# Second feed-forward of an encoder block: four combined pairs of chunks, two block sums of each by accumulating transfers, and the second half of its input copied by ScalarE

## The chip, the cores and the metric

The kernel runs on one core of one Trainium2 chip. Five engines take part: TensorE (PE in the profile, its weight loads PEld), VectorE (DVE), ScalarE (ACT), GpSimd (POOL) and SyncE (SP). SP and POOL issue the DMA transfers used here. The metric is the device time of one execution in microseconds (us); lower is better.

## The reference

One layer of a streaming-encoder block, in single precision, on a sequence of 256 frames of width 1024: a feed-forward, a mixer of a gated recurrence and a forgetting attention, a cross-attention to a memory of 256 frames, and a second feed-forward, each with a norm before and behind it. The change touches only the last step:

```python
def swiglu(h, w_in, w_down):
    gate, up = jnp.split(h @ w_in, 2, axis=-1)
    return (jax.nn.silu(gate) * up) @ w_down
...
        h = rmsnorm(x, ffn2_pre_g[l])
        x = x + 0.5 * rmsnorm(swiglu(h, ffn2_w_in[l], ffn2_w_down[l]), ffn2_post_g[l])
```

Here w_in is 1024 x 5632 and w_down 2816 x 1024.

## The kernel before

**Numbers.** Every fp32 operand is split into a high part (rounded to the fp32r type that TensorE multiplies) and a low part (the rest). ScalarE makes the high part by a cast and VectorE the low part by a subtraction: lines 153 and 155 for a weight tile as it is loaded (`load_split`), 173 and 174 in `split` for all else. A product is three matmuls of 512 columns: high by high, high by low, low by high. A weight tile, a "unit", is 128 x 1024, that is two blocks of 128 rows by 512 columns.

**The feed-forward.** `ffn` is called for both feed-forwards, `f1_in` and `f2_in` in the tables. The hidden width 2816 is cut into 11 chunks of 256 (`NFF`). A chunk's input weights are four units; they give 512 columns, the gates and the ups of the chunk. The 256 frames are two halves (h) of 128. There are three ways to do a chunk. By tokens (`act_tok`, the table `TOKS`): for each half 8 blocks of the width times 3 matmuls, so 24 matmuls, 48 for the chunk. By columns (`act_col`), used for no chunk in question. As a pair with the next chunk (`act_pair`, the table `PAIRS`): the two token halves, the two halves of the width and the two chunks make a 2 x 2 by 2 x 2 block product, which is done in the way of Strassen and Winograd with seven products in place of eight. Each is 12 matmuls, so a pair has 84 where two chunks by tokens have 96. Its price is sums of weight blocks, which are split like weights.

**A pair in order.** `sums` holds block (0, 0) plus further blocks as the pair goes on, `both` a sum of blocks (0, 1) and (1, 1) (the first number is the half of the width, the second tells the chunk, 1 for the pair's first and 0 for its second). Each is two tiles of the "extra" buffers (4 in all); other blocks of a pair are loaded into "raw" buffers (4 in all). The seven products are, with their stationary input: p1 from the plain input, b4 from "de", then on top of p1's bank "aed", on b4's bank "baed", on p1's bank "ad", a new bank b0 from the second half of the width, and "e" on p1's bank. Each is preceded by the splits (`splits`) of two tiles, a cast and a subtraction of 128 x 1024 for either. `add` (line 596) does the block sums on VectorE. `more` (line 569) loads a block; with an operation it is an accumulating transfer issued by POOL, which adds the block to what the tile holds. With `FETCHED` the (1, 1) block comes into `both` that way.

**Outputs.** ScalarE takes copies of p1, v, w and p5, and VectorE combines them to the output quarters c01, c11, c00; the last one is the bank of "e" itself. `act_evac` applies the silu (`sg`, ScalarE, line 450) and multiplies by the up part (`at`, VectorE, lines 453 and 455). `flush` transposes the `at` tiles of a chunk (line 445) and splits them into `acts`, the input of the second product.

**The second product.** `down(c, h)` is 12 matmuls, two of them a chunk. They are put between the products of a pair (`step_between`); the last ones, of chunks 7 to 10, follow at the end. Before, the second feed-forward does chunks 0, 1, 2 by tokens, then pair 3 (chunks 3 and 4, with downs 0 to 2 in between), chunk 5 by tokens, pair 6 (downs 3 to 5), chunk 8 by tokens, and pair 9 (down 6).

**The input.** `X4` is the normed input of the second feed-forward, transposed. Before, it is a `Joined`, with high and low parts side by side, filled by `gain_split` (lines 372 and 373) one 128 x 128 block after another: TensorE transposes four blocks into a bank, ScalarE casts each with the gain of its rows, VectorE subtracts. The second half of the frames is done by `second`, whose transpositions are put in the order among the matmuls of the first half (`after(m + L_F2)`). `pair_joined` adds the parts back together for the pairs, 128 x 512 at a time, and `pair_inputs` forms "de", "aed", "ad", "baed" from that.

**Order.** Instructions of each engine run in a fixed order, made by a scheduler from the order of the code, with `after`, `issue_after` and `high_priority` as bounds. Loads are in SP's order, the accumulating transfers in POOL's.

Of the kernel before, what the change touches and what calls it, by code (L numbers as in the profile page):

```python
# [11 lines left out]
F32 = mybir.dt.float32  # L12
F32R = mybir.dt.float32r
I32 = mybir.dt.int32
AF = mybir.ActivationFunctionType
ALU = mybir.AluOpType
AX = mybir.AxisListType

P = 128
D = 1024  # L20
T = 256
# [11 lines left out]

STAG = 3

TOKS = {"f1_in": (3, 8), "f2_in": (2, 5, 8)}

PAIRS = {"f1_in": (4, 6, 9), "f2_in": (3, 6, 9)}

L_ACT = 21  # L40
L_F1 = 24
# [4 lines left out]
L_F2 = 36  # L46
# [6 lines left out]
M_T = (103, 115)  # L53
M_O = (126, 130)

FETCHED = {"f1_in": (4, 6, 9), "f2_in": (3, 6, 9)}
R_AT = (66, 130, 188, 252, 286, 332)

FG = 3
# [26 lines left out]
def block_kernel(ctx: ExitStack, tc: tile.TileContext, wts, head_in, gf_in, x_in, mem_in, memT_in, cols, rows, fbias, masks, out):  # L86
    nc = tc.nc
    V, S, G, PE = nc.vector, nc.scalar, nc.gpsimd, nc.tensor
# [13 lines left out]
    @contextmanager  # L102
    def after(i):

        with tc.high_priority(), tc.issue_after(log[min(i, len(log) - 1)]):
            yield
# [7 lines left out]
    def m4(shape, dt=F32, n="m"):  # L114
        return mp.tile(shape, dt, tag="m4", name=nm(n))
# [10 lines left out]
    def trp():  # L126
        return pp.tile([P, 512], F32, tag="tr", name=nm("tr"), bufs=2)
# [8 lines left out]
    evicted = []  # L136
# [35 lines left out]
    def split(hi, lo, src):  # L172
        a = S.copy(hi, src)  # L173
        b = V.tensor_tensor(out=lo, in0=src, in1=hi.bitcast(F32), op=ALU.subtract)  # L174
        return a.ins, b.ins

    class Pair:
# [7 lines left out]
        def more(self):  # L185
            self.h.append(m4([P, 4, T], F32R, "hT"))
            self.l.append(m4([P, 4, T], F32R, "lT"))
# [71 lines left out]
    ident = cp.tile([P, P], F32, name="ident")  # L259
# [4 lines left out]
    cols_s = cp.tile([P, 64], F32, name="cols_s")  # L264
# [4 lines left out]
    G_F1, G_MIX, G_MEM, G_KV, G_F2, G_HG, C_LB = 0, 8, 16, 24, 32, 40, 48  # L269
# [63 lines left out]
    def rstd_x(src, into=None, act=False):  # L333

        s = s1(2, name="ss2")
        for j in range(2):
            ssq(s[:, j : j + 1], src[j])
            if act and j == 0:
                b = sums_of(s)
        if not act:  # L340
            return rstd_of(s, into=into)
        r = s1(name="rstd") if into is None else into
        V.tensor_scalar(out=r, in0=step(*root(s, b)), scalar1=-16.0, scalar2=None, op0=ALU.mult)
        return r
# [6 lines left out]
    def fac_of(i, h):  # L351
        return fac[i][:, 32 * h : 32 * h + 1]

    def x_halves(h):
        return [xs[:, h, 0:512], xs[:, h, 512:]]
# [33 lines left out]
    def x_blocks(h):  # L389
        return lambda kb: xs[:, h, kb * P : (kb + 1) * P]  # L390
# [36 lines left out]
    def ffn(w_in, w_dn, X, r2, n_tok, i_row, first_half, second_half=None):  # L427
# [87 lines left out]

        def pair_joined(k):
            t = m4([P, 4, T], n="xf")
            for i in range(2):  # L520
                x = X.t[2 * k + i].bitcast(F32)
                V.tensor_tensor(out=t[:, 2 * i : 2 * i + 2], in0=x[:, :, 0], in1=x[:, :, 1], op=ALU.add)
            return t

        def ratio():

# [44 lines left out]
        def act_pair(c, between):  # L571
            sx, q, more_parts = pairs_in
# [7 lines left out]
            def splits(t):  # L580
                u = []
                for r in t:
                    p = parts_of()
                    split(p[0], p[1], r)
                    u.append(p)
                return u
# [7 lines left out]
            def add(t, o):  # L594
                for x, y in zip(t, o):
                    V.tensor_tensor(out=x, in0=x, in1=y, op=ALU.add)  # L596
# [15 lines left out]
            sums, both = sums_of_pair.pop(c)  # L612
# [19 lines left out]
            raw = raws(1, 1)  # L632
            add(sums, raw)
            u = splits(sums)
            if "e" not in sx:
                more_parts("ad", "e")
            product(b1, of("aed"), u, False)
# [5 lines left out]
            with tc.high_priority():  # L643
                t = half_tile("c01")
# [4 lines left out]
            with tc.high_priority():  # L649
                t = half_tile("c11")  # L650
# [4 lines left out]
            raw = raws(1, 0)  # L655
            m = len(log)
            product(b0, of_x(1), splits(raw), True)
            add(sums, raw)
            with tc.high_priority():
                t = half_tile("c00")  # L660
                V.tensor_tensor(out=t, in0=p1, in1=b0, op=ALU.add)
# [25 lines left out]
        pairs, pairs_in = PAIRS[w_in], None  # L687
        for c in range(n_tok):
            acts[c] = m4([P, 2, 2, T], F32R, "act")
        for h in range(2):  # L690
            m = len(log)
            for c in range(n_tok):
                act_tok(c, h)
            if h == 0 and n_tok:
                second_half(m)
                q, row = ratio()
                if pairs:
                    xf = [pair_joined(k) for k in range(2)]
        accs = None
        done = 0  # L700
        if callable(r2):
# [3 lines left out]
            q, row = ratio()  # L705
# [8 lines left out]
        for c in range(n_tok, NFF):  # L714
# [17 lines left out]
            elif c == 2 and first_half:  # L732
                n = len(log)
# [45 lines left out]
        m = len(log)  # L779
# [68 lines left out]
    def half(X, r, h, g, *ms, into=None, act=True):  # L848

        for i, m in enumerate(ms):  # L850
            with after(m):
                to_T(X, x_blocks(h), h, g, (i,) if len(ms) == 2 else (0, 1), mm if X is X3 and h else trp)
        r[h] = rstd_x(x_halves(h), into, act)
# [537 lines left out]
    def add(t, o):  # L1391
        for x, y in zip(t, o):
            V.tensor_tensor(out=x, in0=x, in1=y, op=ALU.add)  # L1393
# [303 lines left out]
        hold[_AT["mo"] + kb] = marks[(1, 1, 3, 3)[kb]]  # L1697
    for i in range(2):
        place[_AT["f2_in"] + i] = [wp.tile([P, D], F32R, tag="extra", name=nm("w"), bufs=4) for _ in range(2)]
    X4 = Joined()  # L1700
    r4 = [None, None]
    po = [[acc(), acc()], [acc(), acc()]]
    for kb in range(3):
# [12 lines left out]


    def second(m):
        half(X4, r4, 1, G_F2, m + L_F2, into=fac_of(3, 1), act=False)

    ffn("f2_in", "f2_dn", X4, r4, 2, 3, None, second)

# [90 lines left out]
```

## Time and profile before

| | us |
|---|---|
| median of 3 runs | 766.29 |
| the 3 runs | 765.70, 766.29, 767.17 |
| the profiled execution, its own time | 767.82 |
| its span in the profile | 765.6 |
| granted clock, mean | 0.998 |
| TensorE busy | 756.7 (99%) |
| VectorE busy | 664.4 (87%) |
| ScalarE busy | 521.2 (68%) |
| GpSimd busy | 33.0 (4%) |

The profiled execution is one run of its own, and its span leaves out 2.2 us of that time at the start and the end. Busy shares are means over the span; a stage can be bound by another engine than the whole. The chain of waits follows back from the last instruction to what released it. In a group's row stand line, engine and operation, output and inputs by the program's names, shapes, the count, busy us, and the mean ns of one instruction, then the idle time ahead of them and what ended it. In a row of the timeline stand the start in us, the duration, the engine, the line, the operation and, in brackets, the idle time ahead and its releaser.

### The profile page before, as it was taken

Reading aid. Unit: us, or ns where it says so; the run is one execution under the profiler, and the core shown is the slowest. Engines: PE = TensorE matmul, PEld = TensorE weight load, DVE = VectorE, ACT = ScalarE, POOL = GpSimd, SP = SyncE. Lnnn points to the kernel's source line nnn. Section 1 sums busy time; section 2 is a strip of 40 time slices with the busy share of each in tenths; the row PEclk is TensorE's granted clock in tenths of the full one; section 3 lists DMA queues with packets and bytes.
Section 4 is the critical chain, followed back from the end, with each engine's and each line's share of the span. In section 5 each row is a group of like instructions: output and inputs, shape, how many; then the busy total and the mean of one; then the engine's idle time right before and its main releaser. Section 6 shows DMA issues by size and latency. Waiting matters only on the chain.

```text
span 765.6 us, 11756 instructions
## 1 busy us (share of the span) xinstructions
PE 756.7 (99%) x4302; PEld 642.8 (84%) x4302; DVE 664.4 (87%) x982; ACT 521.2 (68%) x841; POOL 33.0 (4%) x56
## 2 busy tenths in 40 slices
PE   9999999999999999999999999999999999999996
PEld 8888888888888998898888888888887888888885
DVE  6799998988678898888689899999979899997973
ACT  8667576688774659667666755875968566675762
POOL 0000000000000100200001000001000100000000
PEclk9999999999999999999999999999999999999999
DMA  9778777674745545835668955586386837868641
GB/s 350 235 259 245 214 239 275 182 252 167 233 158 149 185 137 183 284 128 182 189 220 245 267 183 186 175 286 131 114 291 191 257 108 257 236 222 269 176 131 55
DMA packets 47146, 157.88 MB, mean 206 GB/s; under 512 B 5385, under 2 KB 9105, under 8 KB 47089
## 3 DMA queue, kind: packets, MB, share of 16 engines
q1 hardware_dynamic: 43168, 144.83, 55.5%
q0 software_dynamic: 3488, 11.94, 8.7%
q8 instruction: 33, 0.54, 0.3%
q10 hardware_dynamic: 432, 0.37, 0.2%
q14 instruction: 25, 0.20, 0.1%
HBM read 156.06 MB, written 1.06 MB: 205 GB/s over the span
## 4 chain that ended last, share of the span: by engine, by line
PE 85%; DVE 8%; ACT 2%; DMA 2%; issue 1%; DVEq 0%; ACTq 0%
PE mm L100 45%; PE acc L100 33%; PE tr L100 5%; DVE lo L155 2%; DMA raw<-in_wts_dram 2%; PE tr L445 1%; DVE lo L174 1%; ACT hi L153 1%; PE tr L385 1%; DVE xs L421 1%; DVE sraw L1393 1%; DMA head<-in_head_dram 0%; DVE post L416 0%; DVE sx L174 0%; DVE qm L1578 0%
## 5 line engine op out<-in xcount | busy, mean ns | idle before, releaser
L155 DVE TENSOR_TENSOR lo<-raw,hi 128x1024 fp32r<-128x1024 f32 (+1 forms) x188 | 222.3, 1199 | 29.5 <-ACT hi L153 26.2
L153 ACT CAST hi<-raw 128x1024 fp32r<-128x1024 f32 (+1 forms) x188 | 190.9, 1033 | 50.3 <-DMA raw<-in_wts_dram 29.7
L100 PE MATMUL mm<-hi,hlT 128*128 128x512 f32 (+1 forms) x632 | 191.6, 382 | 0.0
L100 PEld LDWEIGHTS mm<-hi,hlT 128*128 128x128 f32 x632 | 116.7, 188 | 20.2
L100 PE MATMUL mm<-lo,hlT 128*128 128x512 f32 (+1 forms) x316 | 119.1, 381 | 0.0
L100 PE MATMUL acc<-hi,act 128*128 128x512 f32 x352 | 113.6, 390 | 0.0
L173 ACT CAST hi<-sraw 128x1024 fp32r<-128x1024 f32 x80 | 83.3, 1052 | 33.9 <-DVE sraw L596 15.6
L174 DVE TENSOR_TENSOR lo<-sraw,hi 128x1024 fp32r<-128x1024 f32 x80 | 96.1, 1221 | 3.8 <-ACT hi L173 3.4
L100 PE MATMUL mm<-hi,sx 128*128 128x512 f32 x280 | 90.8, 391 | 0.0
L100 PEld LDWEIGHTS acc<-hi,act 128*128 128x128 f32 x352 | 66.2, 188 | 13.4
L100 PE MATMUL acc<-lo,act 128*128 128x512 f32 x176 | 69.5, 395 | 0.0
L100 PEld LDWEIGHTS mm<-lo,hlT 128*128 128x128 f32 x316 | 59.3, 188 | 10.0
L100 PEld LDWEIGHTS mm<-hi,sx 128*128 128x128 f32 x280 | 52.5, 188 | 10.9
L100 PE MATMUL acc<-hlT,hi 128*128 128x512 f32 x240 | 60.7, 394 | 0.0
L100 PE MATMUL mm<-lo,sx 128*128 128x512 f32 x140 | 54.9, 392 | 0.0
L100 PEld LDWEIGHTS acc<-hlT,hi 128*128 128x128 f32 x240 | 43.1, 189 | 7.7 <-DVE hlT L373 0.2
L174 DVE TENSOR_TENSOR lo<-raw,hi 128x1024 fp32r<-128x1024 f32 x32 | 38.6, 1221 | 2.1 <-ACT hi L173 2.0
L173 ACT CAST hi<-raw 128x1024 fp32r<-128x1024 f32 x32 | 33.1, 1053 | 8.5 <-issue 3.1
L100 PEld LDWEIGHTS acc<-lo,act 128*128 128x128 f32 x176 | 33.1, 188 | 6.4
L100 PE MATMUL acc<-lo,hT 128*128 128x512 f32 x96 | 37.8, 393 | 0.0
L100 PE MATMUL acc<-hi,hT 128*128 128x512 f32 x96 | 37.7, 392 | 0.1
L100 PE MATMUL acc<-hi,lT 128*128 128x512 f32 x96 | 37.3, 391 | 0.0
(329 smaller groups left out, 1232.4 us busy)
## 6 DMA issues: line engine op xcount, KB each, us to landing
raw<-in_wts_dram SPq DMA_DIRECT2D x215, 512.0 KB, 4.6
sraw<-in_wts_dram SPq DMA_DIRECT2D x32, 512.0 KB, 6.6
sraw<-in_wts_dram POOLq DMA_DIRECT2D x20, 512.0 KB, 5.9
raw<-in_gf_dram SPq DMA_DIRECT2D x12, 344.0 KB, 3.7
head<-in_head_dram SPq DMA_DIRECT2D x7, 392.0 KB, 6.4
grow<-in_rows_dram SPq DMA_DIRECT2D x4, 512.0 KB, 7.6
xs<-in_x_dram SPq DMA_DIRECT2D x2, 512.0 KB, 7.6
cb<-cd POOLq DMA_DIRECT2D x2, 512.0 KB, 4.9
```

Of the source, the lines that this page charges most:

```text
L100: log.append(PE.matmul(*args, **kw).ins)
L153: casts.append(S.copy(h, r).ins)
L155: los.append(V.tensor_tensor(out=l, in0=r, in1=h.bitcast(F32), op=ALU.subtract).ins)
L173: a = S.copy(hi, src)
L174: b = V.tensor_tensor(out=lo, in0=src, in1=hi.bitcast(F32), op=ALU.subtract)
L385: PE.transpose(blocks[-1][1], src(kb), ident)
L421: summed = V.scalar_tensor_tensor(out=xh, in0=ts[a // 512][:, a % 512 : (b - 1) % 512 + 1], scalar=r, in1=xh, op0=ALU.mult, op1=ALU.add)
L445: PE.transpose(trv[:, j, h * P : (h + 1) * P], ats[c, h][:, j * P : (j + 1) * P], ident)
L1393: V.tensor_tensor(out=x, in0=x, in1=y, op=ALU.add)
```

## The change

In the second feed-forward the chunks 5 and 8 are no longer done by tokens: chunks 3 to 10 are four pairs, 3, 5, 7 and 9. Pair 3 has the downs 0 to 2 in between, pair 5 the downs 3 and 4, pair 7 the downs 5 and 6, and pair 9 none. In each pair the block (1, 0) is added to `sums` by an accumulating transfer of POOL, issued behind the splits for "aed" (`FETCHED_LAST`), where VectorE added a loaded copy. `X4` is a `Pair`, with the high and the low parts in tiles of their own. `second` now transposes a block, lets ScalarE copy it with its gain to an fp32 tile `xf4`, and splits four blocks at once. `joined` writes the first half of `xf4` as the sum of high and low parts, one instruction for four blocks.

```diff
--- before.py
+++ after.py
@@ -33,9 +33,9 @@
 
 STAG = 3
 
-TOKS = {"f1_in": (3, 8), "f2_in": (2, 5, 8)}
-
-PAIRS = {"f1_in": (4, 6, 9), "f2_in": (3, 6, 9)}
+TOKS = {"f1_in": (3, 8), "f2_in": (2,)}
+
+PAIRS = {"f1_in": (4, 6, 9), "f2_in": (3, 5, 7, 9)}
 
 L_ACT = 21
 L_F1 = 24
@@ -53,7 +53,8 @@
 M_T = (103, 115)
 M_O = (126, 130)
 
-FETCHED = {"f1_in": (4, 6, 9), "f2_in": (3, 6, 9)}
+FETCHED = {"f1_in": (4, 6, 9), "f2_in": (3, 5, 7, 9)}
+FETCHED_LAST = {"f1_in": (), "f2_in": (3, 5, 7, 9)}
 R_AT = (66, 130, 188, 252, 286, 332)
 
 FG = 3
@@ -515,12 +516,9 @@
 
 
 
-        def pair_joined(k):
-            t = m4([P, 4, T], n="xf")
-            for i in range(2):
-                x = X.t[2 * k + i].bitcast(F32)
-                V.tensor_tensor(out=t[:, 2 * i : 2 * i + 2], in0=x[:, :, 0], in1=x[:, :, 1], op=ALU.add)
-            return t
+        def joined(k):
+            hi, lo = (t[k].bitcast(F32)[:, :, :P] for t in (X.h, X.l))
+            V.tensor_tensor(out=xf4[k][:, :, :P], in0=hi, in1=lo, op=ALU.add)
 
         def ratio():
 
@@ -632,6 +630,9 @@
             raw = raws(1, 1)
             add(sums, raw)
             u = splits(sums)
+            if c in FETCHED_LAST[w_in]:
+                for j in range(2):
+                    more(sums[j], c, 1, 0, j, ALU.add)
             if "e" not in sx:
                 more_parts("ad", "e")
             product(b1, of("aed"), u, False)
@@ -655,7 +656,8 @@
             raw = raws(1, 0)
             m = len(log)
             product(b0, of_x(1), splits(raw), True)
-            add(sums, raw)
+            if c not in FETCHED_LAST[w_in]:
+                add(sums, raw)
             with tc.high_priority():
                 t = half_tile("c00")
                 V.tensor_tensor(out=t, in0=p1, in1=b0, op=ALU.add)
@@ -694,8 +696,9 @@
             if h == 0 and n_tok:
                 second_half(m)
                 q, row = ratio()
-                if pairs:
-                    xf = [pair_joined(k) for k in range(2)]
+                xf = xf4
+                for k in range(2):
+                    joined(k)
         accs = None
         done = 0
         if callable(r2):
@@ -1697,7 +1700,8 @@
         hold[_AT["mo"] + kb] = marks[(1, 1, 3, 3)[kb]]
     for i in range(2):
         place[_AT["f2_in"] + i] = [wp.tile([P, D], F32R, tag="extra", name=nm("w"), bufs=4) for _ in range(2)]
-    X4 = Joined()
+    X4 = Pair()
+    xf4 = [m4([P, 4, T], n="xf") for _ in range(2)]
     r4 = [None, None]
     po = [[acc(), acc()], [acc(), acc()]]
     for kb in range(3):
@@ -1716,7 +1720,16 @@
 
 
     def second(m):
-        half(X4, r4, 1, G_F2, m + L_F2, into=fac_of(3, 1), act=False)
+        for q in range(2):
+            x = xf4[q][:, :, P:]
+            ps = trp()
+            with after(m + L_F2):
+                for j in range(4):
+                    kb = 4 * q + j
+                    PE.transpose(ps[:, j * P : (j + 1) * P], x_blocks(1)(kb), ident)
+                    S.activation(x[:, j], ps[:, j * P : (j + 1) * P], AF.Copy, scale=cols_s[:, G_F2 + kb : G_F2 + kb + 1])
+                evicted.append(split(X4.h[q][:, :, P:], X4.l[q][:, :, P:], x))
+        r4[1] = rstd_x(x_halves(1), fac_of(3, 1))
 
     ffn("f2_in", "f2_dn", X4, r4, 2, 3, None, second)
 
```

The order of instructions moves at three places. In the rows, numbers behind names tell tiles of one name apart.

TensorE where the second half of the input is made, `tr` being the banks of the transpositions, `mm` the bank of the first half's chunk 1. Before:

```order
L100 MATMUL mm_6239<-hi_6253,hlT_5960 128x512
L385 MATMUL tr_6292<-ident,xs 128x128 x4
L385 MATMUL tr_6297<-ident,xs 128x128 x4
L100 MATMUL mm_6239<-lo_6254,hlT_5960 128x512
L100 MATMUL mm_6239<-hi_6253,hlT_5960 128x512 x2
```

Now:

```order
L101 MATMUL mm_6241<-hi_6255,hT_5960 128x512
L1729 MATMUL tr_6294<-ident,xs 128x128
L1729 MATMUL tr_6305<-ident,xs 128x128
L101 MATMUL mm_6241<-lo_6256,hT_5960 128x512
L101 MATMUL mm_6241<-hi_6255,lT_5961 128x512
L1729 MATMUL tr_6294<-ident,xs 128x128
L101 MATMUL mm_6241<-hi_6255,hT_5960 128x512
L1729 MATMUL tr_6305<-ident,xs 128x128
```

Eight transpositions stood together; now the two banks take turns, with matmuls in between.

VectorE at the start of pair 9. Before, 7354 and 7356 are pair 9's `sums`, 7358 and 7360 its `both`:

```order
L174 TENSOR_TENSOR lo_7418<-sraw_7354,hi_7417 128x1024
L596 TENSOR_TENSOR sraw_7354<-sraw_7354,raw_7457 128x1024
L174 TENSOR_TENSOR lo_7422<-sraw_7356,hi_7421 128x1024
L174 TENSOR_TENSOR lo_7464<-sraw_7354,hi_7463 128x1024
L453 TENSOR_TENSOR at_7352<-mm_7325,sg_7350 128x256
L596 TENSOR_TENSOR sraw_7356<-sraw_7356,raw_7458 128x1024
L596 TENSOR_TENSOR sraw_7354<-sraw_7354,raw_7538 128x1024
L174 TENSOR_TENSOR lo_7468<-sraw_7356,hi_7467 128x1024
```

Now, 7415 and 7417 are its `sums`; the `at` tile 7413 is of pair 7's last product:

```order
L454 TENSOR_TENSOR at_7382<-c_1562_7378,sg_7380 128x256
L175 TENSOR_TENSOR act_7140<-tr_7404,act_7140 128x512
L456 SCALAR_TENSOR_TENSOR at_7413<-mm_7144,q_6334,sg_7411 128x256
L175 TENSOR_TENSOR lo_7462<-sraw_7415,hi_7461 128x1024
L175 TENSOR_TENSOR lo_7466<-sraw_7417,hi_7465 128x1024
L594 TENSOR_TENSOR sraw_7415<-sraw_7415,raw_7482 128x1024
L175 TENSOR_TENSOR act_7141<-tr_7449,act_7141 128x512
L594 TENSOR_TENSOR sraw_7417<-sraw_7417,raw_7483 128x1024
L175 TENSOR_TENSOR lo_7489<-sraw_7415,hi_7488 128x1024
L175 TENSOR_TENSOR lo_7493<-sraw_7417,hi_7492 128x1024
```

The splits for b4 and "aed" with the sum between them stood around the last `at` of chunk 8; now all of them stand behind the last `at` of pair 7.

ScalarE at the end, behind the copy `pc` of pair 9. Before:

```order
L450 ACTIVATE sg_7533<-c_1592_7531,facs 128x256
L153 CAST hi_7673<-raw_7672 128x1024
L450 ACTIVATE sg_7566<-c_1602_7564,facs 128x256
L173 CAST act_7362<-tr_7590 128x512
L153 CAST hi_7682<-raw_7681 128x1024
L450 ACTIVATE sg_7597<-mm_7366,facs 128x256
```

Now:

```order
L451 ACTIVATE sg_7560<-c_1608_7558,facs 128x256
L154 CAST hi_7671<-raw_7670 128x1024
L154 CAST hi_7680<-raw_7679 128x1024
L451 ACTIVATE sg_7591<-c_1618_7589,facs 128x256
L174 CAST act_7423<-tr_7615 128x512
L451 ACTIVATE sg_7622<-mm_7427,facs 128x256
```

One cast of a reloaded down weight stood between the silus of c11 and c00; now there are two.

## The prediction

> **What bounds the kernel now.** I read the page's busy line and the chain of waits first, then both feed-forwards by stage, then single instructions around the pairs.
>
> ```profile
> span 765.6 us, 11756 instructions
> ...
> PE 756.7 (99%) x4302; PEld 642.8 (84%) x4302; DVE 664.4 (87%) x982; ACT 521.2 (68%) x841; POOL 33.0 (4%) x56
> ...
> PE 85%; DVE 8%; ACT 2%; DMA 2%; issue 1%; DVEq 0%; ACTq 0%
> ```
>
> TensorE is busy 99% and carries 85% of the chain. So a matmul taken out is time gained, as long as VectorE, at 87% second, still hands over its operands in time. Busy time by stage says how near it is. The columns are the stretch, its length, then busy time (and instructions) of PE, weight loads, DVE, ACT and POOL, the granted clock, the DMA share and GB/s. The first two stretches are pair 4 and what follows it in the first feed-forward; the last two lie in the second.
>
> ```profile
> 56.00:95.00 39.00, 39.00 (x179) 32.29 (x178) 37.79 (x41) 26.19 (x34) 1.97 (x3) 1.00 0.77 226
> 95.00:130.00 35.00, 35.00 (x160) 28.96 (x159) 32.22 (x35) 25.56 (x32) 0.00 (x0) 1.00 0.82 278
> 665.00:700.00 35.00, 35.00 (x162) 29.01 (x161) 30.44 (x32) 24.53 (x31) 0.00 (x0) 1.00 0.77 260
> 700.00:740.00 40.00, 39.68 (x181) 32.63 (x180) 38.13 (x41) 28.77 (x37) 1.69 (x2) 1.00 0.63 184
> ```
>
> TensorE has almost no gap, but around the pairs VectorE is 38.13/40 = 95% busy and in the first row 97%. A pair trades matmuls for VectorE work, and the change puts four of them almost end to end. What VectorE does there:
>
> ```profile
> L155 DVE TENSOR_TENSOR lo<-raw,hi 128x1024 fp32r<-128x1024 f32 x176 | 212.1, 1221 | 27.1 <-ACT hi L153 23.9 <-PE acc L100 1.3 <-PE tr L100 1.2
> L174 DVE TENSOR_TENSOR lo<-sraw,hi 128x1024 fp32r<-128x1024 f32 x80 | 96.1, 1221 | 3.8 <-ACT hi L173 3.4
> ...
> L596 DVE TENSOR_TENSOR sraw<-sraw,raw 128x1024 f32<-128x1024 f32 x24 | 28.8, 1221 | 1.4 <-DMA raw<-in_wts_dram 1.3
> ```
>
> A subtraction for a low part and a block sum cost the same, 1.221 us. Back to back they overlap a little:
>
> ```profile
> 722.19 1.22 DVE L174 TENSOR_TENSOR lo<-raw,hi 128x1024 fp32r<-128x1024 f32 x1
> 723.33 0.69 DVE L174 TENSOR_TENSOR act<-tr,act 128x512 fp32r<-128x512 f32 x1
> 723.93 1.22 DVE L174 TENSOR_TENSOR lo<-raw,hi 128x1024 fp32r<-128x1024 f32 x1
> 725.06 1.22 DVE L174 TENSOR_TENSOR lo<-sraw,hi 128x1024 fp32r<-128x1024 f32 x1
> ```
>
> The starts give a step of 725.06 - 723.93 = 1.13 to 1.14 us for 1024 columns and 0.60 for 512. For TensorE one row of the chain suffices, 24 matmuls in 5.44 us, 0.2267 each:
>
> ```profile
> 634.95 5.44 PE mm L100 x24
> ```
>
> **The sum.** It is made against the profiled execution's own 767.82 us (span 765.6 and 2.2 around it), which is 1.53 over the median of 766.29.
>
> *Matmuls removed.* Six chunks in three pairs and chunks 2, 5, 8 by tokens become eight chunks in four pairs and chunk 2 by tokens. Two chunks by tokens are 2 x 48 = 96 matmuls, a pair 7 x 12 = 84: 12 fewer, 12 x 0.2267 = **-2.72**.
>
> *The old wait at the end.* Before, the last transpositions of pair 9 wait for VectorE's final product `at`:
>
> ```profile
> PE tr L445 <- DVE at L455: 0.3, 1, 0.3
> ```
>
> That 0.3 goes with the old order: **-0.3**. What stands there instead is the last term.
>
> *The entry.* Now eight transpositions run as one group:
>
> ```profile
> 589.14 1.03 PE L385 MATMUL tr<-ident,xs 128*128 128x128 f32 x8
> 590.98 0.62 ACT L372 ACTIVATE hlT<-tr,cols_s 128x128 fp32r<-128x128 f32 x2
> 592.33 0.60 DVE L373 SCALAR_TENSOR_TENSOR hlT<-tr,cols_s,hlT 128x128 fp32r<-128x128 f32 x2
> 592.53 0.84 PE L100 MATMUL mm<-w,hlT 128*128 128x512 f32 x3
> ```
>
> In the change each transposition of a bank waits until ScalarE has copied the one before it, so the eight go one by one between matmuls. The first product of the second half then needs a whole four-block cast and the VectorE subtraction behind it, where two 128x128 blocks did. The row that resembles that split (of a pair's input, same shape) is
>
> ```profile
> 620.68 0.62 ACT L173 CAST sx<-ss 128x512 fp32r<-128x512 f32 x1 [2.78 <-DVE ss L541]
> 621.77 0.69 DVE L174 TENSOR_TENSOR sx<-ss,sx 128x512 fp32r<-128x512 f32 x1
> ```
>
> 621.77 + 0.69 - 620.68 = 1.8 us from the cast's start to the end of the low part. At best the copies are early and only the longer subtraction shows (0.69 against 0.60/2 = 0.3 for one block: 0.3 with rounding); at worst the whole 1.8 lies behind the last copy. The transpositions come about ten matmuls ahead of the first use, which hides part; I take a little over the middle, **+1.2** (0.3 to 1.8). VectorE gives back four 512-column adds for two joined ones, off the path.
>
> *The seams 3-5, 5-7, 7-9.* Before, a chunk by tokens stood between two pairs of the second feed-forward. After the last product of a pair the silu and `at` must be done before its transpositions, which come 6 matmuls (1.36 us) into the next pair's first product. The times of that step, here at pair 3:
>
> ```profile
> 651.57 0.39 PE L100 MATMUL mm<-hi,hlT 128*128 128x512 f32 x1
> 651.77 0.48 ACT L450 ACTIVATE sg<-mm,facs 128x256 f32<-128x256 f32 x1 [0.95 <-PE mm L100]
> 652.14 1.04 ACT L153 CAST hi<-raw 128x1024 fp32r<-128x1024 f32 x1
> 652.30 0.48 DVE L455 SCALAR_TENSOR_TENSOR at<-mm,q,sg 128x256 f32<-128x256 f32 x1
> ```
>
> With the stage's edge at 651.57 the silu starts at +0.20, the next cast at +0.57, `at` at +0.73, ending at +1.21, in time for +1.36. The first feed-forward has such a seam, pair 4 to pair 6:
>
> ```profile
> 92.71 0.48 DVE L455 SCALAR_TENSOR_TENSOR at<-mm,q,sg 128x256 f32<-128x256 f32 x1
> ```
>
> ```profile
> 93.65 0.44 PE tr L445 x4
> ```
>
> There VectorE is 93.65 - 92.71 - 0.48 = 0.46 ahead, with 12 matmuls of a down product (2.72) in the seam that the second one will lack; two block sums fewer give back 2 x 1.135 = 2.27. 0.46 - 2.72 + 2.27 is zero. At worst VectorE is one step (1.135) late once. I take **+0.3** (0 to 1.3) for the three. The accumulating transfers themselves I cost at nothing: POOL is 4% busy, and the pairs' down products hide the landing; what that costs without cover is rival D.
>
> *Pair 9.* The largest term. A pair is 18 steps of 1.135 (14 low parts, 4 sums), 3 of 0.60 for its output halves, four `at` of about 0.36 and two low parts of activations of 0.60: 24.9 us of VectorE, against 84 x 0.2267 = 19.0 and two groups of transpositions, 19.9, on TensorE. Two down chunks add 10.9 us to TensorE and only 4 steps to VectorE, which evens it out (30.8 against 29.4). Pairs 5 and 7 take the downs of chunks 3 to 6, so pair 9 has none. Before, it had one, and its first splits were made under chunk 8. In VectorE's new order the following stand behind `at` of pair 7, counted from the start of pair 9's first product: `at` 0.73; the second product's low parts, whose cast ScalarE starts at 0.57 and ends at 1.61, at 1.65 and 2.79; a block sum 3.92; an activation's low part 5.06; the other sum 5.66; the third product's low part 6.79, ready at 8.02. TensorE has 12 matmuls and 4 transpositions (3.16), then 12 (5.88), and its second matmul of the third product, the first that reads that low part, could start at 6.11. It waits **+1.9**. Nothing in the queue can be passed, as the order is fixed; behind the waiting matmul stands all of TensorE. A gain of VectorE on pair 7 cannot shorten it, since `at` depends on TensorE's last product. The bounds are 0, if the first half of the low part comes free sooner than the steps say, and 2.2, with both ahead-standing sums at the full 1.22.
>
> *The last downs.* The downs of chunks 7 to 10 come after the last pair, before and now. Two rows of the old end give the prices:
>
> ```profile
> 730.59 4.57 DMA raw<-in_wts_dram
> ```
>
> ```profile
> 735.26 1.05 ACT L153 CAST hi<-raw 128x1024 fp32r<-128x1024 f32 x1 [1.40 <-DMA raw<-in_wts_dram]
> ```
>
> A reload takes 4.57 us after VectorE frees its buffer, and a cast that waited 1.40 for one already holds up the silu behind it. In the change VectorE reaches the end later by its 24.9 - 19.9 = 5.0 us of surplus, less the 1.9 that TensorE waits; two such casts now stand ahead of the third silu. Following both queues from row to row I get 0.6 at the second unit of down 7, 0.55 and 0.4 at chunk 9's transpositions and low part, 0.4 at chunk 10's: **+2.0** (0 to 2.2).
>
> Sum: -2.72 - 0.3 + 1.2 + 0.3 + 1.9 + 2.0 = +2.4. 767.82 + 2.4 = 770.2 on the profiled execution's own time, and on the median 766.29 + 2.4 = **768.7**. A measurement here tells about 0.2%, 1.5 us, from no change: the forecast is slower, though by little more than that.
>
> **The rivals.**
>
> *B: only the rigid wait is paid.* The leads that the shorter block sums give cover entry, seams and end. -3.0 + 1.9, and 0.3 at least at the entry: -0.8, 765.5; with half the end's 2.0, 766.5. For it: each pair loses two of its sums on VectorE (2.27), and before only 0.3 us of waiting for `at` showed. Against: the end's reload is a latency that no lead in VectorE shortens. This is the case on the other side, no change: it decides if the reloads of downs 7 and 8 land before TensorE's last pair product ends.
>
> *C: all hidden.* -3.0, 763.3. For it: the first feed-forward runs two pairs end to end without a gap (row 56 to 95). Against: that one has its downs in between, and pair 9 has none.
>
> *D: the accumulating transfers land late.* The change adds ten of POOL's transfers.
>
> ```profile
> L569 POOL DMA_DIRECT2D sraw<-in_wts_dram x12: 839/850/887, 54.3 to 705.3; - x12
> ...
> DMA to landing us min/median/max: 5.2/6.5/10.2
> ```
>
> The issue takes 0.85 us, the landing 6.5 (5.2 to 10.2). In pair 9 the sum is free at 8.0; 0.85 + 6.5 + 1.05 for the cast + 1.2 for the low part make 17.6, while TensorE needs it in its seventh product, at about 18.9 by the times above. A landing of 10.2 eats this 1.3 and costs 3.7 - 1.3 = 2.4: 771.1, and with pair 7 too 773.5. It decides from a landing of 7.8 on. Against: the median of the twelve is 6.5, pairs 3, 5 and 7 have downs as cover, and the issue's spread, 839 to 887 ns, shows no blocking although VectorE is 95% busy around it.
>
> The Trainium skill, page "SBUF — State Buffer", section "🔬 SBUF: two separate sides", warns that a transfer issued by GpSimd has its descriptors written by GpSimd's own cores, which a VectorE operation of the two-port kind locks out, so that the transfer seems blocked; it speaks against this change. By that rule the landings would stretch by a VectorE operation or more as VectorE fills up, towards case D; the trace shows landings of up to 10.2 us, but an issue within 48 ns.
>
> **How the numbers follow.** A 0.50, B 0.25, C 0.13, D 0.12. A's own range is 767.3 (entry and end at half) to 770.5. C's last microsecond and D's upper half are left out, which gives 764.4 to 771.8. Slower by over 0.2% are A and D, 0.62; within it B, 0.25; faster C, 0.13.
>
> **What would show it.** After 589 us: a gap of TensorE ahead of the second half's first product (1.2), none of over 0.5 at the seams, one of 1.9 ahead of pair 9's third product with VectorE's subtraction as releaser, and some 2 us of short waits after the last pair, for casts on reloads. VectorE should be busy over 95% from pair 7 on. I am wrong if pair 9 runs through, which would be C, if the stalls lie at seams, or if a row names a POOL transfer as what TensorE's operands waited for.

## The result, and the profile after

The change made the kernel slower: 779.63 us (median of 4 runs, 777.61 to 781.74) against 766.73 beside it, a ratio of 1.0164 (95% interval 1.0141 to 1.0187). The forecast was slower, 768.7 with a range up to 771.8; the loss is about 13 us where 2.4 were forecast. The profiled execution took 780.16.

The page after, span, busy line, chain by engine and then the software DMA queue (packets, MB, share of 16 engines' span):

```profile
span 778.4 us, 11781 instructions
...
PE 759.9 (98%) x4290; PEld 639.7 (82%) x4290; DVE 669.2 (86%) x981; ACT 529.7 (68%) x853; POOL 41.6 (5%) x66
...
q0 software_dynamic: 4928, 17.18, 12.5%
...
PE 61%; DVE 18%; DMA 11%; ACT 5%; issue 4%; DVEq 0%; POOL 0%; ACTq 0%; SPq 0%; POOLq 0%
```

TensorE lost its hold on the chain: 61% where it had 85%, and DMA, 2% before, has 11%. VectorE's busy time grew by 4.8 us and TensorE's by 3.2, while the span grew by 12.8. So TensorE's idle time grew by 9.6, and most of the loss is waits. The timeline of TensorE after has these longer gaps behind the entry (0.61 there), with what ended each in brackets:

```profile
658.16 0.44 PE L446 MATMUL tr<-ident,at 128*128 128x128 f32 x2 [2.83 <-DVE at L456]
692.18 0.44 PE L446 MATMUL tr<-ident,at 128*128 128x128 f32 x2 [1.09 <-DVE at L456]
724.23 0.44 PE L446 MATMUL tr<-ident,at 128*128 128x128 f32 x2 [0.69 <-DVE at L454]
725.36 0.44 PE L446 MATMUL tr<-ident,at 128*128 128x128 f32 x2 [0.70 <-DVE at L456]
731.95 0.50 PE L101 MATMUL mm<-lo,sx 128*128 128x512 f32 x1 [1.23 <-DVE lo L175]
750.03 0.50 PE L101 MATMUL acc<-lo,act 128*128 128x512 f32 x1 [0.77 <-DVE lo L156]
```

The first four are the seams 3-5, 5-7 and 7-9, which all wait for `at`. With smaller gaps (0.23 at the first seam, 0.41 in pair 7) they come to about 6 us. Pair 9's third product waits 1.23, and 0.31 ahead of that; the last row is of the last downs. Why `at` is late at the first seam is read from the chain of waits after:

```profile
632.21 7.85 DMA raw<-in_wts_dram
...
640.14 1.06 ACT hi L174
...
645.34 6.11 DMA sraw<-in_wts_dram
...
651.54 1.22 DVE sraw L594
...
657.62 0.49 DVE at L456
...
658.16 0.44 PE tr L446 x2
```

A plain load of a raw block takes 7.85 us to land, against a median of 4.7 for such loads over the run; the load of a sum behind it takes 6.11 (such loads have a median of 6.2). Pairs 5 and 7 have a raw block's load of 7.81 and 8.68 in the chain, too. VectorE sits idle for both, in the middle of a pair in which it has little to spare: 2.15 us and 1.49 us by its timeline.

```profile
641.22 2.36 DVE L175 TENSOR_TENSOR lo<-raw,hi 128x1024 fp32r<-128x1024 f32 x2 [2.15 <-ACT hi L174]
...
651.54 1.23 DVE L594 TENSOR_TENSOR sraw<-sraw,sraw 128x1024 f32<-128x1024 f32 x1 [1.49 <-DMA sraw<-in_wts_dram]
```

The same shows over all pairs in the groups of instructions, of before first and of after below (behind the second bar, the idle time ahead of the group and what ended it):

```profile
L174 DVE TENSOR_TENSOR lo<-raw,hi 128x1024 fp32r<-128x1024 f32 x32 | 38.6, 1221 | 2.1 <-ACT hi L173 2.0
```

```profile
L175 DVE TENSOR_TENSOR lo<-raw,hi 128x1024 fp32r<-128x1024 f32 x36 | 43.3, 1223 | 12.3 <-ACT hi L174 12.2
```

Ahead of the raw blocks' low parts VectorE idles 12.3 us where it idled 2.1. It waits for ScalarE's casts, and those wait for the loads.

### The profile page after: what moved, and what is told of

It is laid out like the page before. It is cut to its first block, busy times and chain, and to the rows that moved or that the text cites. A ratio compares the mean times of both kernels' runs of the same rounds, so it can differ in the third digit from the quotient of the medians.

```text
span 778.4 us, 11781 instructions
## 1 busy us (share of the span) xinstructions
PE 759.9 (98%) x4290; PEld 639.7 (82%) x4290; DVE 669.2 (86%) x981; ACT 529.7 (68%) x853; POOL 41.6 (5%) x66
## 3 DMA queue, kind: packets, MB, share of 16 engines
q0 software_dynamic: 4928, 17.18, 12.5%
## 4 chain that ended last, share of the span: by engine, by line
PE 61%; DVE 18%; DMA 11%; ACT 5%; issue 4%; DVEq 0%; POOL 0%; ACTq 0%; SPq 0%; POOLq 0%
PE mm L101 32%; PE acc L101 23%; DMA raw<-in_wts_dram 7%; DVE lo L156 4%; PE tr L101 4%; DVE lo L175 4%; ACT hi L154 2%; DMA sraw<-in_wts_dram 2%; DVE sraw L594 2%; ACT hi L174 1%; DMA row<-rd 1%; PE tr L446 1%; DVE sx L175 1%; DVE sraw L1396 1%; DVE xs L422 1%
## 5 line engine op out<-in xcount | busy, mean ns | idle before, releaser
L156 DVE TENSOR_TENSOR lo<-raw,hi 128x1024 fp32r<-128x1024 f32 (+1 forms) x180 | 212.7, 1198 | 30.4 <-ACT hi L154 27.1
L154 ACT CAST hi<-raw 128x1024 fp32r<-128x1024 f32 (+1 forms) x180 | 182.4, 1032 | 50.0 <-DMA raw<-in_wts_dram 29.7
L101 PE MATMUL mm<-hi,hlT 128*128 128x512 f32 (+1 forms) x464 | 138.4, 378 | 0.0
L174 ACT CAST hi<-sraw 128x1024 fp32r<-128x1024 f32 x90 | 92.9, 1051 | 32.5 <-DVE sraw L594 16.5
L175 DVE TENSOR_TENSOR lo<-sraw,hi 128x1024 fp32r<-128x1024 f32 x90 | 107.9, 1221 | 2.8 <-ACT hi L174 2.4
L101 PE MATMUL mm<-hi,sx 128*128 128x512 f32 x320 | 104.4, 392 | 1.2 <-ACT pc L649 0.5
L101 PEld LDWEIGHTS mm<-hi,hlT 128*128 128x128 f32 x464 | 85.2, 188 | 13.8
L101 PE MATMUL mm<-lo,hlT 128*128 128x512 f32 (+1 forms) x232 | 86.3, 377 | 0.0
L101 PE MATMUL mm<-lo,sx 128*128 128x512 f32 x160 | 63.0, 394 | 1.2 <-DVE lo L175 1.2
L175 DVE TENSOR_TENSOR lo<-raw,hi 128x1024 fp32r<-128x1024 f32 x36 | 43.3, 1223 | 12.3 <-ACT hi L174 12.2
L101 PEld LDWEIGHTS mm<-lo,hlT 128*128 128x128 f32 x232 | 43.5, 188 | 6.8
```

Of the source, the lines that this page charges most:

```text
L101: log.append(PE.matmul(*args, **kw).ins)
L154: casts.append(S.copy(h, r).ins)
L156: los.append(V.tensor_tensor(out=l, in0=r, in1=h.bitcast(F32), op=ALU.subtract).ins)
```

## The experiments

The change has three parts: the new second half of the input, four pairs for three, and the accumulating transfers of block (1, 0). They were taken apart first. Numbers are medians, with the ratio to the kernel before on the same chip and its 95% interval.

**The new second half alone** (`TOKS`, `PAIRS` and `FETCHED` of the second feed-forward as before, no accumulating transfer of block (1, 0); shown in part):

```diff
-FETCHED_LAST = {"f1_in": (), "f2_in": (3, 5, 7, 9)}
+FETCHED_LAST = {"f1_in": (), "f2_in": ()}
-PAIRS = {"f1_in": (4, 6, 9), "f2_in": (3, 5, 7, 9)}
+PAIRS = {"f1_in": (4, 6, 9), "f2_in": (3, 6, 9)}
```

> The new second half of the input alone, with the three pairs, the chunks 2, 5, 8 by tokens and VectorE's block sums of before. Theory S (the loss sits at the seams between pairs, where VectorE's queue waits for the reload of a block sum): only the entry is paid, the 1.6 us by which the first activation's transpositions come later in the changed kernel, so 768.3. Rival E (the copied second half pushes VectorE late and all later stalls start there): most of the 12.9 us stays, 775 or more.

768.26 against 767.53, 1.0009 (0.9999 to 1.0019): no difference that can be told. The entry isn't where the time went.

**Four pairs alone** (the tables of the change in the kernel before; `FETCHED` goes with them and is left out here):

```diff
-TOKS = {"f1_in": (3, 8), "f2_in": (2, 5, 8)}
+TOKS = {"f1_in": (3, 8), "f2_in": (2,)}
-PAIRS = {"f1_in": (4, 6, 9), "f2_in": (3, 6, 9)}
+PAIRS = {"f1_in": (4, 6, 9), "f2_in": (3, 5, 7, 9)}
```

> Four pairs alone, with the old second half and with block (1, 0) added by VectorE, not by an accumulating transfer. Theory S: the seams are there and VectorE has two sums more in each pair, 4 x 2.27 = 9 us more work, partly in its idle time: 776 to 784. Rival E: near 767, since the second half is the old one. Rival A (the accumulating transfers of the block (1, 0) land late and stretch each pair): clearly faster than the change, 768 to 772.

774.91, 1.0089 (1.0072 to 1.0107). Just below the range of the first theory and above that of the accumulating transfers. The gaps are different ones: one seam of 1.01 and, in pair 9, four waits of 0.75 and more.

```profile
723.77 0.51 PE L100 MATMUL mm<-hi,sx 128*128 128x512 f32 x1 [1.62 <-ACT hi L173]
725.02 0.50 PE L100 MATMUL mm<-lo,sx 128*128 128x512 f32 x1 [0.75 <-DVE lo L174]
736.91 0.49 PE L100 MATMUL mm<-hi,sx 128*128 128x512 f32 x1 [0.95 <-ACT hi L173]
739.37 0.50 PE L100 MATMUL mm<-lo,sx 128*128 128x512 f32 x1 [1.97 <-DVE lo L174]
```

So in this kernel, without the accumulating transfers, the seams nearly run through, though VectorE has two sums more in each pair, and pair 9, which has no downs, pays.

**The order at the seams.** The sum that waited for its load stood ahead of `at` in VectorE's queue. It was put behind:

```diff
-            add(sums, both)
+            with tc.issue_after(evs[-1][1]) if c - 2 in pairs else nullcontext():
+                add(sums, both)
```

> The change with one edit: in a pair that follows a pair, the sum of block (0, 0) and the other block is issued behind the last product `at` of the pair before, so that no waiting sum stands ahead of `at` in VectorE's queue. Theory S: the seams' waits of about 8 us (4.8, 1.3, 1.8) fall under 2, while pair 9 pays some 1.7 more for two sums that now stand behind `at`: about 775. Rival V (VectorE simply has too much work there, in whatever order): no change, 778 to 781.

779.24, 1.0147 (1.0131 to 1.0163): no gain. The seam 3-5 has no gap any more, but around 5-7 there are three (0.50, 1.35, 0.56) and pair 9 and the end wait longer. In this run the order changed where the lateness comes out, not how much there is of it.

**Buffers for the second sum.** Its load had to wait until the last product's split freed its buffers:

```diff
-                r = wp.tile([P, D], F32, tag="extra", name=nm("sraw"), bufs=4)
+                r = m4([P, D], n="sraw") if n and w_in == "f2_in" else wp.tile([P, D], F32, tag="extra", name=nm("sraw"), bufs=4)
```

> The change with one edit: the second sum of a pair (blocks (0, 1) and (1, 1)) is loaded into buffers of its own from the data pool and no longer into those that the split for the last product must free. Theory S: its load can land before the sum needs it, the seams go, and what is left is the entry 1.6, pair 9 about 3 and the end 2.0 against the 3.0 gained: 770 to 773. Rival V: no change, 778 to 781.

793.57, 1.0335 (1.0316 to 1.0354), far outside either expectation. The edit moved other loads and the order of every engine but GpSimd too, and raw blocks in its chain of waits landed after 8.0 to 8.4 us. It doesn't tell the theories apart, and whether more buffers would help in the old order stays open.

**The accumulating transfers.** The next two kernels keep the order of the change on every engine, and both leave part of the last product's sum out. In one the transfers are plain, in the other they are gone.

```diff
                 for j in range(2):
-                    more(sums[j], c, 1, 0, j, ALU.add)
+                    G.dma_start(sums[j], wts[_AT[w_in] + 4 * (c + 1) + 2 + j - 4])
```

> The change, with the accumulating transfers of block (1, 0) turned into plain ones from the same queue: same blocks, same bytes, same order on every engine. The sum for the last product of each pair is left out (it holds block (1, 0) alone). Theory A: an accumulating transfer keeps the 16 DMA engines busy for twice the time of a plain one, (12.5% of 778.4 - 8.7% of 765.6)/10 = 3.1 us against 55.5% of 765.6 x 0.52/144.8 = 1.5; the loads of the raw blocks behind them land at 7.8 in place of 4.7, VectorE idles for them and reaches the seams late. Then 8 x 1.5 = 12 us of DMA time goes, and some 4 to 8 of it shows: 771 to 776. Rival R (the reload waits on buffers that VectorE frees late, whatever moves): no change, 778 to 781.

772.12, 1.0056 (1.0039 to 1.0073): 7.5 us faster than the change. The seams' gaps are 0.55 and 0.75 and then none. The software queue's row, with as many packets and bytes as in the change:

```profile
q0 software_dynamic: 4928, 17.18, 11.3%
```

```diff
-            if c in FETCHED_LAST[w_in]:
-                for j in range(2):
-                    more(sums[j], c, 1, 0, j, ALU.add)
```

> The change without any transfer of block (1, 0) into the sums: the last product of each pair lacks that block. Theory A: 8 x 3.1 us less on the DMA engines, and no landing ahead of the last split: 768 to 772, the 3.0 of the matmuls against entry, pair 9 and end. Rival R: 776 to 780.

771.24, 1.0048 (1.0032 to 1.0064), and VectorE's idle time ahead of the raw blocks is back at what it was before:

```profile
q0 software_dynamic: 3776, 12.99, 9.5%
```

```profile
L175 DVE TENSOR_TENSOR lo<-raw,hi 128x1024 fp32r<-128x1024 f32 x36 | 43.1, 1221 | 2.1 <-ACT hi L174 1.8
```

With plain transfers that idle time is 6.6 us, and the kernel takes only 0.9 more than with none, so part of the idle time costs nothing. By the ratios to the kernel before, plain transfers give back 8.3 us of the change's time, and leaving them out 8.9.

From the three rows of the queue and the spans (778.4, 769.0 and 769.9) a transfer's price on all 16 engines follows: accumulating (12.5% x 778.4 - 9.5% x 769.9)/8 = 3.0 us, plain (11.3% x 769.0 - 9.5% x 769.9)/8 = 1.7 us. The same bytes cost 1.3 us more when they are added.

**VectorE's sums in place of the transfers:**

```diff
-FETCHED_LAST = {"f1_in": (), "f2_in": (3, 5, 7, 9)}
+FETCHED_LAST = {"f1_in": (), "f2_in": ()}
```

> The change with block (1, 0) added by VectorE as before, in all four pairs, so eight accumulating transfers fewer and 8 x 1.14 = 9 us more for VectorE. Theory A: as the four pairs alone with the old input (774.9), plus 0 to 1.6 for the entry: 774 to 777. Rival V (VectorE's load decides): above the change, 782 or more.

777.22, 1.0131 (1.0113 to 1.0149), just above theory A's range. Its seams have gaps of 1.11, 0.56 and 0.47. Against the kernel with neither, VectorE's eight sums cost 6.0 us and the eight transfers 8.4: the transfers are dearer by 2.4, at the edge of what two such runs can tell. So the transfers alone don't make the four pairs slow: a kernel with complete sums pays in either way.

**Held up on the DMA engines, or waited for?** Both the plain transfer and none at all also shorten the wait for the sum itself. So the transfers were sent at the same point into tiles that nobody reads:

```diff
                 for j in range(2):
-                    more(sums[j], c, 1, 0, j, ALU.add)
+                    aside = xf[j].rearrange("p a b -> p (a b)")
+                    G.tensor_copy(out=aside[:, :1], in_=u[j][1][:, :1].bitcast(F32))
+                    more(aside, c, 1, 0, j, ALU.add)
```

> The change with its accumulating transfers of block (1, 0) sent at the same point of GpSimd's queue, the same size, but into two spare tiles that nothing reads; the sums lack that block, as in the run without the transfers, and the order on every other engine is that of the change. GpSimd copies one column of the low part ahead of each, so that they start when they did. Theory O (they hold up the plain loads behind them on the DMA engines): 776 to 780, as the change. Rival W (what costs is that the last product's split waits for the sum to land): 770 to 773, as without the transfers.

792.26, 1.0335 (1.0307 to 1.0363): spoilt by its own edit. In pair 3 those tiles were still to be read, and VectorE waited 11.7 us for them. Repeated in pairs 5, 7 and 9 alone (`and c > 3` in the condition), with a control that keeps the one-column copies and drops the transfers:

> As the transfers into spare tiles, but in pairs 5, 7 and 9 alone, since in pair 3 those tiles were still to be read and VectorE waited 11.7 us for them. No sum holds block (1, 0). Theory O (accumulating transfers hold up the plain loads behind them on the DMA engines): the seams 5-7 and 7-9 wait as in the change (1.3 and 1.8 us), the time is 773 to 777. Rival W (only a split that waits for the sum's own landing costs): no seam waits beyond those without the transfers (1.5 and 0), the time 770 to 772.5.

> The control: GpSimd's one-column copies of the run with the transfers into spare tiles, without the transfers. No sum holds block (1, 0). Both theories: as the run without the transfers, 770 to 772.5; if it is slower, the copies cost and the run with the transfers has to be read against this one.

With the transfers 779.51, 1.0160 (1.0140 to 1.0180); the control 771.32, 1.0045 (1.0028 to 1.0062). Six transfers that nothing waits for cost 8.2 us, as much as the change's eight. The time is above theory O's range too (773 to 777), and far from rival W's; some 3.4 of the 8.2 are two stretches of a lower clock behind waits (last section). Time to landing of the plain loads of blocks (min, median, max) between 600 and 745 us, in the run with the transfers and in the control:

```profile
DMA to landing us min/median/max: 3.0/6.4/9.9
```

```profile
DMA to landing us min/median/max: 3.1/5.0/7.4
```

And the seam 5-7, in the same order:

```profile
687.67 0.44 PE L446 MATMUL tr<-ident,at 128*128 128x128 f32 x2 [1.54 <-DVE at L454]
689.80 0.44 PE L446 MATMUL tr<-ident,at 128*128 128x128 f32 x2 [1.46 <-DVE at L456]
```

```profile
687.88 0.44 PE L446 MATMUL tr<-ident,at 128*128 128x128 f32 x2 [1.05 <-DVE at L456]
```

The plain loads land 1.4 us later in the median, and TensorE waits at the seam for it. So what costs is what these transfers do to the loads behind them; the sum's own landing isn't needed for it. That it is time on the DMA engines fits the queue's rows (3.0 us against 1.7 for the same packets). No run separates it from anything else that the transfers and the loads may share.

**Pair 3's transfers left out** (VectorE adds there):

```diff
-FETCHED_LAST = {"f1_in": (), "f2_in": (3, 5, 7, 9)}
+FETCHED_LAST = {"f1_in": (), "f2_in": (5, 7, 9)}
```

> The change with block (1, 0) added by VectorE in pair 3 alone and by accumulating transfers in pairs 5, 7 and 9. Theory O: pair 3's transfers go, so the seam 3-5 falls from 3.4 us and the lower clock behind it (1.4) to the 1.3 that VectorE's sums left; the seams 5-7 and 7-9 stay: 774 to 777. Rival: a late VectorE only moves the loss to the next seam, 778 to 780.

776.55, 1.0127 (1.0097 to 1.0157), as theory O has it (the profiled execution took 780.31, so its gaps are those of a longer one). The seam 3-5 falls to a gap of 0.88. The seam 5-7 has 0.98 and 1.46, 7-9 has 1.52 and 0.69, more than in the change, so part of the loss did move on.

**Transfers behind the raw loads** (they are taken out where they stood, which is not shown):

```diff
             raw = raws(1, 0)
+            for j in range(2):
+                with tc.issue_after(loads[-1]):
+                    more(sums[j], c, 1, 0, j, ALU.add)
```

> The change with its accumulating transfers of block (1, 0) issued behind the two plain loads of the same pair's last raw block, where they stood ahead of them. Theory A (they hold up the plain loads behind them on the DMA engines, VectorE idles for those and comes late to the seam): the raw loads land at about 4 in place of 7.8, the seams' 8 us fall to about 2: 771 to 775. Rival Q (whatever stands behind them is held up, now the loads of the next pair's sums): 777 to 781.

779.67, 1.0159 (1.0141 to 1.0176), but the edit did not do what it says. GpSimd still issued first, since the bound holds in the scheduler's order only and SyncE's loads waited for their buffers:

```profile
630.47 1.74 POOL L567 DMA_DIRECT2D sraw<-in_wts_dram  x2 [21.62 <-ACT hi L174]
```

```profile
632.24 2.67 SPq L565 DMA_DIRECT2D raw<-in_wts_dram  x2
```

Whether a true hold would help wasn't tried.

**Pair 9.** The down of chunk 7 was moved into pair 9, in the four pairs alone, in the kernel just shown, and in four pairs with the old second half and the accumulating transfer in pair 9 only (the edit in part; the loops over the last downs start at `tail`):

```diff
-                downs = [(i, h) for i in range(done, min(c, NFF - STAG - 1)) for h in range(2)]
+                tail = NFF - STAG + (w_in == "f2_in")
+                upto = tail - 1 if c == NFF - 2 else NFF - STAG - 1
+                downs = [(i, h) for i in range(done, min(c, upto)) for h in range(2)]
```

> Four pairs with VectorE's sums and the old second half, and the down of chunk 7 moved from the end into pair 9, which had none: 5.4 us more on TensorE there against two VectorE steps. In the four pairs alone TensorE waited 5.5 us in pair 9 and 1.2 at the seams. Theory P (pair 9 without cover costs 5): most of that goes, 769 to 771. Rival: the wait moves to the end, where a down less covers the last silu: 774 to 776.

770.25, 1.0038 (1.0025 to 1.0051), 4.7 us less than the four pairs alone (3.9 by the ratios). What is left in pair 9 is one wait of 2.08 us and a short one of 0.34.

> As the kernel with the accumulating transfers issued late, and with the down of chunk 7 moved from the end into pair 9, which gained 4.7 us in the four pairs with VectorE's sums. Theory: pair 9's wait of 2.0 to 2.6 goes here too, and little else: 768 to 772. Rival: with accumulating transfers pair 9's wait is already short and the end pays: no gain over the run without the move.

776.83, 1.0132 (1.0115 to 1.0149): a miss, only 2.8 us less than without the move, since the seams keep their waits and the last product waits 1.03 for a copy of ScalarE's (so does the next kernel).

> Four pairs with the old second half, the down of chunk 7 in pair 9, VectorE's sums in pairs 3, 5 and 7 and the accumulating transfer of block (1, 0) in pair 9 alone. The run without that transfer has 770.3, of which TensorE waits 2.2 in pair 9 for the last product's low part behind VectorE's sums and loses about 1.5 to a lower clock behind it. Theory A: a transfer where the DMA engines have room costs nothing and takes that wait away: 766.5 to 768, even with the kernel before. Rival: the transfer lands late there, 770 or more.

769.62, 1.0031 (1.0019 to 1.0042): a miss too. The wait for the low part went, but the last product then waits 1.57 us for a copy of ScalarE. That copy stands behind a cast which waited 3.33 us for the landing of the sum itself, which is the rival's cause, if not its time:

```profile
737.52 1.04 ACT L174 CAST hi<-sraw 128x1024 fp32r<-128x1024 f32 x1 [3.33 <-DMA sraw<-in_wts_dram]
```

No version here beats the kernel before.

## Why the prediction was wrong

The direction was right, the range was not. Step by step:

- Matmuls removed, -2.72: 4290 matmul records for 4302, as counted.
- The entry, +1.2: the first transpositions of an activation come at 604.98 us where they came at 603.42, so 1.6 in the trace; the part alone moved the median by 0.7, within its interval of -0.1 to 1.5. About right in size, in part by luck: the gap of 0.61 and most of the rest lie between the transpositions, each of which waits for ScalarE's copy of the one before. Ahead of the second half's first product, where the prediction looked for the wait, there is about 0.2.
- The seams, +0.3 (0 to 1.3): this term failed. The gaps there are 0.23 + 2.83 + 1.09 + 0.69 + 0.70 = 5.5 us, and 1.7 more went by a lower clock behind the longest (last section). Stalls at the seams are what the prediction had named as a sign against itself. Even without the transfers the term is short: the seams' gaps are 2.0 in the kernel that leaves block (1, 0) out and 2.1 with VectorE's sums.
- Pair 9, +1.9: 0.31 + 1.23 = 1.5 us ahead of and in the third product, and 0.47 before the last. The queue of VectorE was read rightly, and the moved down (4.7 us in the four pairs) shows that pair 9 without downs is what costs there.
- The last downs, +2.0: gaps of 0.26, 0.77 and 0.38, so 1.4. A term of the right kind.

The step that failed under the seams' term is the sentence "The accumulating transfers themselves I cost at nothing: POOL is 4% busy, and the pairs' down products hide the landing; what that costs without cover is rival D." It looked at the engine that issues and at who waits for the landing. What the transfers use up is time of the 16 DMA engines, 3.0 us each by the queue's row, and plain loads issued within a few us behind them land later; those loads are on VectorE's path, through ScalarE's cast, in a pair with little to spare (30.8 us of TensorE against 29.4 of VectorE in the prediction's own budget). Plain transfers in their place gave back 7.5 us, none 8.4, and transfers that nobody reads took 8.2.

Case D named the right part of the change, and gave it 2.4 us at one or two places, since it priced only the landing of the sum itself. In the change that wait shows once, in pair 9, where ScalarE waits 2.2 us for the transfer and the copy `pc` behind it comes 0.47 late for TensorE (1.57 in the kernel with the transfer in pair 9 alone):

```profile
741.83 1.05 ACT L174 CAST hi<-sraw 128x1024 fp32r<-128x1024 f32 x1 [2.22 <-DMA sraw<-in_wts_dram]
```

The page of the Trainium skill cited there, "SBUF — State Buffer", section "🔬 SBUF: two separate sides", has GpSimd locked out of writing descriptors while VectorE runs an operation of the two-port kind; no run shows that for these transfers, whose issue stays at 0.84 to 0.88 us in the change's second feed-forward. Nor would it tell a plain transfer from an accumulating one, and the plain ones from the same queue cost 0.9 us in all. The delay is behind the issue.

The forecast without this term would have been near: without the transfers of block (1, 0) the kernel takes 771.2, at the upper part of the range. But that kernel leaves the block out, and its terms miss both ways (seams 2.0 for 0.3, pair 9 1.5 for 1.9, the last downs 1.0 for 2.0), so this nearness is in part luck. Beside that, A's own range comes to 767.1 to 770.8 by its terms, not 767.3 to 770.5, which changes nothing here.

The sum of the parts isn't closed. Gaps of 10.0 us in all against 0.3 before, 1.7 for the clock and -2.7 for the matmuls make 8.7 of the 12.8 by which the span grew. The entry's transpositions one by one have 1.0 beyond its gap. The rest, some 3 us, wasn't taken apart. It may lie at the edges of the 13 gaps: a gap is counted from the end of the matmul ahead, 0.39 after its start and not 0.23, and behind the gap the second matmul starts 0.34 after the first (750.03 and 750.37), which makes some 0.27 a gap, 3.5 in all, an estimate.

## What to carry to other kernels

Price a DMA transfer on the DMA engines, from the queue's row of bytes and share, and ask which loads are issued behind it and who needs them; an idle issuing engine says nothing of that. An accumulating transfer is dearer than its bytes, here 3.0 us against 1.7, so it is worth a VectorE sum of 1.2 us only where the loads behind it have slack. Here, in a stage whose second engine had 5% left, loads that were a few microseconds late became waits of the first engine at the next point where the two meet.

## What the hardware showed that was not expected

A wait of TensorE cost more than itself. Behind the gap of 2.83 us the granted clock fell, and matmuls came 0.43 us apart for a while, where 0.2267 is usual. The stretches of 4 us after it (the number behind POOL's count is the granted clock):

```profile
656.00:660.00 4.00, 1.84 (x7) 1.53 (x8) 4.00 (x5) 0.64 (x1) 0.05 (x1) 0.88 1.02 207
660.00:664.00 4.00, 4.00 (x14) 3.16 (x13) 3.66 (x5) 2.27 (x4) 0.00 (x0) 0.70 0.91 289
664.00:668.00 4.00, 4.00 (x19) 3.31 (x18) 3.96 (x4) 3.65 (x5) 1.70 (x2) 1.00 0.39 42
```

0.12 x 4 + 0.30 x 4 = 1.7 us were lost so. The Trainium skill, page "TensorE: Matmul & The Clock Gate", section "🔬 Part 1: The HAM clock gate (the "warmup" mystery)", has a half-rate clock set when TensorE was idle for a window of about 3.4 us. The half rate agrees with the spacing here (0.43 us for 512 columns), and 1.7 us lost at half rate are a stretch of 3.4; the gap was shorter than the window, 2.83 with 0.23 just before, and a single one of 2.08 in the four pairs with the moved down had the same effect, while one of 1.83 us had none.

The length alone doesn't decide it. Gaps of 0.95 and 1.97 in pair 9 brought a granted clock of 0.78 behind them with VectorE's sums and the new second half, and none below 1.00 in the four pairs alone. Gaps of 0.31 and 1.23 in pair 9 had no such effect in the change, but did in the run with the transfers into spare tiles in pairs 5, 7 and 9, which has a second such stretch behind a gap of 1.97:

```profile
728.00:732.00 4.00, 2.99 (x7) 2.35 (x8) 3.97 (x4) 3.80 (x4) 2.68 (x3) 0.65 0.00 0
732.00:736.00 4.00, 4.00 (x18) 3.24 (x17) 2.63 (x3) 2.57 (x4) 1.38 (x2) 0.92 0.97 205
748.00:752.00 4.00, 3.44 (x12) 2.91 (x13) 4.00 (x6) 2.62 (x4) 0.00 (x0) 0.71 0.50 151
752.00:756.00 4.00, 4.00 (x16) 3.18 (x16) 3.53 (x4) 2.17 (x3) 0.00 (x0) 0.86 0.75 243
```

Together they lose 1.4 + 0.3 + 1.2 + 0.6, about 3.4 us; its control has a clock of 1.00 from 600 us to the end of its matmuls. So part of a difference between two such kernels can be whether a wait brings the lower clock or not.

GpSimd's copy of one column in the first run with the spare tiles took 6.18 us the first time, while VectorE was busy without a gap, 0.49 right behind that, and 1.2 to 1.6 us in later pairs:

```profile
629.97 6.18 POOL L636 COPY xf<-lo 128x1 f32<-128x1 f32 x1 [20.92 <-DVE lo L175]
```
